# Eight weight buffers as tiles of their own, with 64 bytes between each two

## The chip, the cores and the metric

The kernel runs on one core of a Trainium2 chip, as one launch. The metric is the device time of that launch in microseconds (us), as the median of several runs; smaller is better. A profile is one further execution, taken by the hardware profiler. Engines are named as the profile names them: PE is TensorE's matrix multiply, PEld its weight load, DVE is VectorE, ACT is ScalarE, POOL is GpSimd, SP issues the DMAs.

## The reference

Four layers over 256 tokens of width 1024, batch 1, in float32. Each layer is a half-weighted SwiGLU block, a mixer (three kinds in turn: dilated attention with three groups, differential attention, sliding-window attention with sinks), and a second half-weighted SwiGLU block, each between two RMS norms:

```
def swiglu(x, w_gate, w_up, w_down):
    return (jax.nn.silu(x @ w_gate) * (x @ w_up)) @ w_down

for i in range(DEPTH):                      # DEPTH = 4, D_FF = 2816
    f = swiglu(rms_norm(x, norm_pre[i, 0]), ...)
    x = x + FFN_HALF * rms_norm(f, norm_post[i, 0])
    m = mixer_i(rms_norm(x, norm_pre[i, 1]))
    x = x + rms_norm(m, norm_post[i, 1])
    f = swiglu(rms_norm(x, norm_pre[i, 2]), ...)
    x = x + FFN_HALF * rms_norm(f, norm_post[i, 2])
```

Nearly all arithmetic is in products of the 256 token rows with weights, and every weight is used once per launch.

## The kernel before

**Split products.** Each float32 factor is written as the sum of a high part, rounded to the multiplier's one-pass float32 type, and a low part, the rest. A product then takes three matmuls into the same accumulator: high by high, high by low and low by high (`mm3`, lines 175 to 177). In a matmul one operand is stationary (128 columns, loaded by PEld) and the other streams past it (256, 384 or 512 columns). In the FFN blocks and the output projections the weights stream and the transposed activations are stationary; in the mixers' query and key projections (`qk`) the weights are stationary and the activations stream.

**Weights.** All weights are one list of 377 units of up to 128 x 2048 float32, that is 8 KB per partition each, in the order of use. `load_next` fetches a unit into one of three `raw` buffers by a DMA from SP. `split_next` makes the unit's two parts: ACT copies `raw` into `hi` with rounding (line 142), then DVE subtracts `hi` from `raw` into `lo` (line 143); units in `on_pool` have that subtraction on POOL. A unit is cut into two pieces (four for the first two units and for POOL's). `hi` and `lo` each have four buffers (`AHEAD = 4`). When the last matmul on a unit has been written down, `done` and `pump` split and load the next one, so a unit waits for the buffer of the unit four before it. The framework sets the semaphores, and orders each engine's instructions by the program's order and given priorities.

**Where things lie in SBUF.** Pools follow one another in the order in which they are opened, and in a pool the tags in the order in which they are first asked for. `wp` holds `raw` (3 x 8 KB), `hi` (4 x 8 KB) and `lo` (4 x 8 KB), without gaps. `actp` follows with `x` (8 KB), a gain (4 KB), three work tiles `w` (4 KB each, the transposed probabilities `pw` of the first mixer among them), `xTh` and `xTl` (8 KB each, the transposed input of a block, high and low) and a second gain (4 KB). So all buffers of `raw`, `hi`, `lo`, `xTh` and `xTl` lie whole multiples of 8 KB apart. Behind them the pool `small` has 62 slots of 32 bytes, that is 64 bytes less than a multiple of 512, and then come the block's own tiles: `hTh` and `hTl` (the transposed hidden values, stationary for the down projection `acc`), `oTh` and `oTl`, and the attention's `vh`, `vl`, `q`, `k`. Their distance from `hi`, `lo`, `xTh`, `xTl` and `pw` is therefore 64 bytes off a multiple of 512.

**Names in the profile.** `gu`, `g` and `u` are gate and up projections (weights stream past `xTh`, `xTl`), `acc` the down and output projections (weights stream past `hTh`, `hTl` or `oTh`, `oTl`), `lead` and `v` projections of a mixer with streaming weights, `qk` those with stationary weights. `sc` and `o` are the attention's own products without weights, `tp` a transpose.

Of the kernel before, what the change touches and what calls it, by code (L numbers as in the profile page):

```python
# [8 lines left out]
F32 = mybir.dt.float32  # L9
F32R = mybir.dt.float32r  # L10
# [4 lines left out]
P = 128  # L15
# [9 lines left out]
AHEAD = 4  # L25
# [21 lines left out]
def tile_network(  # L47
# [28 lines left out]
    act, dve, pe, pool = nc.scalar, nc.vector, nc.tensor, nc.gpsimd  # L76

    const = ctx.enter_context(tc.tile_pool(name="const", bufs=1))
    wp = ctx.enter_context(tc.tile_pool(name="wp", bufs=AHEAD))
# [35 lines left out]
    def load_next():  # L115
# [8 lines left out]
            nc.sync.dma_start(out=t[:, c:c + n], in_=units[i][:, c:c + n])  # L124
        raws[i] = t

    def split_next():
        i = state["split"]
        if i >= NU:
            return  # L130
        state["split"] += 1
        w = units[i].shape[-1]
        r = raws.pop(i)
        hi = wp.tile([P, 2048], F32R, tag="hi", name="hi")
        lo = wp.tile([P, 2048], F32R, tag="lo", name="lo")
        eng = pool if i in on_pool else dve
        pieces = 4 if i < 2 or i in on_pool else PIECES
        n = w // pieces
        if True:
            for c in range(pieces):  # L140
                cs = slice(c * n, (c + 1) * n)
                act.copy(out=hi[:, cs], in_=r[:, cs])  # L142
                eng.tensor_tensor(out=lo[:, cs], in0=r[:, cs], in1=hi[:, cs].bitcast(F32), op=ALU.subtract)  # L143
        his[i], los[i] = hi, lo
# [8 lines left out]
    def pump(n=99):  # L153
        while pending and n:
            n -= 1
            i = pending.pop(0)
            split_next()
            load_next()
            for f in hooks.pop(i, []):
                f()  # L160
# [59 lines left out]
    def norm_elem(t, s, parts=1):  # L220

        ss = small.tile([P, 1], F32, tag="ssx", name="ssx")
        hn = actp.tile([P, D], F32, tag="w", name="hn", bufs=3)
        act.activation(out=hn, in_=x[:, t], func=AF.Square, scale=1.0 / 32.0, accum_out=ss)
        r = rstd_of(ss, None)
        for c in range(parts):
            cs = slice(c * D // parts, (c + 1) * D // parts)
            i = dve.scalar_tensor_tensor(out=hn[:, cs], in0=x[:, t, cs], scalar=r, in1=gains["pre", s][:, cs],
                                     op0=ALU.mult, op1=ALU.mult)
        hn_of[t] = hn  # L230
        return i
# [732 lines left out]
    if True:  # L964
# [10 lines left out]
        with tc.high_priority(PRI):  # L975
            i = norm_elem(0, 0, 2)
            j = norm_tr(0)
        with tc.issue_after(i.ins):
            split_next()
# [3 lines left out]
        for _ in range(AHEAD - 1):  # L983
            split_next()
            load_next()
# [158 lines left out]
```

## Time and profile before

| | |
|---|---|
| median of 3 runs | 2353.83 us (2352.81 to 2354.49) |
| the profiled execution | 2352.16 us, of which its span is 2350.3 us |
| granted TensorE clock, mean of the span | 0.991 of full speed |
| PE busy | 2295.6 us (98%), 12922 matmuls |
| weight loads busy | 2016.5 us (86%) |
| DVE, ACT, POOL busy | 1303.9, 1202.3, 619.2 us |
| HBM read | 401.56 MB |

Busy time of PE counts a matmul from its start to its modelled end, and matmuls overlap; the step from one matmul's start to the next one's says more of its pace than its duration does. Idle time of an engine that nobody waits for costs nothing.

### The profile page before, as it was taken

What the parts mean: (1) busy time and instruction counts of PE and PEld (TensorE: products, weight loads), DVE (VectorE), ACT (ScalarE), POOL (GpSimd) and SP (SyncE); (2) the same over time, 40 slices, a digit from 0 to 9 for tenths busy, and PEclk for the clock granted to TensorE, in tenths of its full rate; (3) what the DMA queues carried; (4) which work ended last, traced back from release to release, by engine and by line L of the source; (5) the groups of instructions that cost most, each with busy time, mean ns of one, the idle gap of its engine ahead of it and who ended that gap; (6) DMA issues with size and microseconds to landing.
All of it is one profiled execution on the core that took longest, in us unless ns stands there. A gap on an engine that the chain in (4) does not pass through costs nothing.

```text
span 2350.3 us, 32498 instructions
## 1 busy us (share of the span) xinstructions
PE 2295.6 (98%) x12922; PEld 2016.5 (86%) x12922; DVE 1303.9 (55%) x1914; ACT 1202.3 (51%) x2109; POOL 619.2 (26%) x590
## 2 busy tenths in 40 slices
PE   8999999999999998899999997999999999999998
PEld 6889999988888888788888886788888899998887
DVE  6545444565465558865465459655555544446553
ACT  5435666554444446554454447544444466665442
POOL 0005877620020027520020033100200277774000
PEclk9999999999999999999999998999999999999999
DMA  7544434354554544155555542455455453443542
GB/s 284 194 175 171 168 147 155 140 197 182 187 204 179 182 180 144 73 215 184 192 197 182 189 153 90 161 185 188 168 214 186 173 189 142 146 153 135 215 179 90
DMA packets 60776, 404.71 MB, mean 172 GB/s; under 512 B 7120, under 2 KB 8144, under 8 KB 16592
## 3 DMA queue, kind: packets, MB, share of 16 engines
q1 hardware_dynamic: 60480, 402.57, 46.9%
q8 instruction: 101, 1.65, 0.3%
q14 instruction: 51, 0.42, 0.1%
q10 hardware_dynamic: 144, 0.07, 0.0%
HBM read 401.56 MB, written 1.05 MB: 171 GB/s over the span
## 4 chain that ended last, share of the span: by engine, by line
PE 91%; DVE 6%; ACT 2%; DMA 1%; issue 1%; POOL 0%; SPq 0%; POOLq 0%; DVEq 0%; ACTq 0%
PE gu L177 11%; PE gu L176 11%; PE gu L175 11%; PE acc L175 8%; PE acc L176 8%; PE acc L177 7%; PE qk L175 4%; PE qk L177 4%; PE qk L176 4%; PE v L175 2%; PE v L177 2%; PE v L176 2%; PE tp L367 2%; PE tp L781 1%; PE u L175 1%; PE u L176 1%
## 5 line engine op out<-in xcount | busy, mean ns | idle before, releaser
L142 ACT CAST hi<-raw 128x1024 fp32r<-128x1024 f32 (+2 forms) x970 | 774.5, 843 | 771.7 <-PE gu L177 323.0
L143 DVE TENSOR_TENSOR lo<-raw,hi 128x1024 fp32r<-128x1024 f32 (+1 forms) x546 | 659.5, 1246 | 553.4 <-ACT hi L142 553.2
L143 POOL TENSOR_TENSOR lo<-raw,hi 128x512 fp32r<-128x512 f32 (+1 forms) x424 | 547.0, 1323 | 206.2 <-ACT hi L142 201.6
L175 PE MATMUL gu<-hi,xTh 128*128 128x512 f32 (+1 forms) x1280 | 474.2, 370 | 0.0
L177 PE MATMUL gu<-hi,xTl 128*128 128x512 f32 (+1 forms) x1280 | 471.3, 368 | 0.0
L176 PE MATMUL gu<-lo,xTh 128*128 128x512 f32 (+1 forms) x1280 | 471.0, 368 | 0.0
L213 POOL TENSOR_SCALAR ms<-ssf 128x1 f32<-128x1 f32 x24 | 8.3, 347 | 1413.1 <-ACT junk L242 1410.1
L176 PE MATMUL acc<-lo,hTh 128*128 128x512 f32 x704 | 279.0, 396 | 0.0
L175 PE MATMUL acc<-hi,hTh 128*128 128x512 f32 x704 | 277.1, 394 | 0.0
L177 PEld LDWEIGHTS gu<-hi,xTl 128*128 128x128 f32 x1280 | 241.3, 188 | 40.0
L177 PE MATMUL acc<-hi,hTl 128*128 128x512 f32 x704 | 275.5, 391 | 0.0
L175 PEld LDWEIGHTS gu<-hi,xTh 128*128 128x128 f32 x1280 | 241.4, 189 | 39.3
L176 PEld LDWEIGHTS gu<-lo,xTh 128*128 128x128 f32 x1280 | 241.4, 189 | 39.0
L175 PE MATMUL qk<-xTh,hi 128*128 128x256 f32 x800 | 229.5, 287 | 0.0
L177 PE MATMUL qk<-xTh,lo 128*128 128x256 f32 x800 | 226.6, 283 | 0.0
L176 PE MATMUL qk<-xTl,hi 128*128 128x256 f32 x800 | 226.5, 283 | 0.0
L177 PEld LDWEIGHTS acc<-hi,hTl 128*128 128x128 f32 x704 | 132.2, 188 | 29.9
L175 PEld LDWEIGHTS acc<-hi,hTh 128*128 128x128 f32 x704 | 132.3, 188 | 29.2
L176 PEld LDWEIGHTS acc<-lo,hTh 128*128 128x128 f32 x704 | 132.4, 188 | 26.9
L176 PEld LDWEIGHTS qk<-xTl,hi 128*128 128x128 f32 x800 | 153.4, 192 | 0.0
L177 PEld LDWEIGHTS qk<-xTh,lo 128*128 128x128 f32 x800 | 153.3, 192 | 0.0
L175 PEld LDWEIGHTS qk<-xTh,hi 128*128 128x128 f32 x800 | 153.3, 192 | 0.0
(200 smaller groups left out, 3399.6 us busy)
## 6 DMA issues: line engine op xcount, KB each, us to landing
raw<-in_w_ffn_dram SPq DMA_DIRECT2D x263, 1024.0 KB, 4.8
raw<-in_w_a_qk_dram SPq DMA_DIRECT2D x48, 1024.0 KB, 4.8
raw<-in_w_a_v_dram SPq DMA_DIRECT2D x32, 768.0 KB, 4.3
raw<-in_w_a_out_dram SPq DMA_DIRECT2D x8, 1024.0 KB, 4.8
raw<-in_w_b_qk_dram SPq DMA_DIRECT2D x8, 1024.0 KB, 4.8
gain<-in_g_pre_dram SPq DMA_DIRECT2D x12, 512.0 KB, 6.3
gain<-in_g_post_dram SPq DMA_DIRECT2D x12, 512.0 KB, 8.4
raw<-in_w_b_v_dram SPq DMA_DIRECT2D x4, 1024.0 KB, 4.8
```

The source lines that it names most:

```text
L142: act.copy(out=hi[:, cs], in_=r[:, cs])
L143: eng.tensor_tensor(out=lo[:, cs], in0=r[:, cs], in1=hi[:, cs].bitcast(F32), op=ALU.subtract)
L175: pe.matmul(o, lhsT=a[0], rhs=b[0], start=first, stop=False)
L176: pe.matmul(o, lhsT=a[0], rhs=b[1], start=False, stop=False)
L177: pe.matmul(o, lhsT=a[1], rhs=b[0], start=False, stop=last)
L213: pool.tensor_scalar(out=ms, in0=a, scalar1=b, scalar2=EPS, op0=ALU.add, op1=ALU.add)
L367: pe.transpose(tp[:, i * P:(i + 1) * P], h[:, i * P:(i + 1) * P], ident)
L781: pe.transpose(tp[:, c0:c0 + P], sp[:, i * P:(i + 1) * P], ident)
```

## The change

The four `hi` buffers and the four `lo` buffers stop being slots of two tags and become eight tiles with a tag and a single buffer each, chosen by the unit's number modulo four. When a buffer is first asked for, a 64-byte tile is asked for behind it (16 float32 per partition), and POOL sets it to zero once. Nothing else is edited.

```diff
+    spaces = set()
+
+    def spaced(tag):
+
+        if tag not in spaces:
+            spaces.add(tag)
+            pool.memset(wp.tile([P, 16], F32, tag=tag, name="pad", bufs=1), 0.0)
+
     def split_next():
...
-        hi = wp.tile([P, 2048], F32R, tag="hi", name="hi")
-        lo = wp.tile([P, 2048], F32R, tag="lo", name="lo")
+        b = i % AHEAD
+        hi = wp.tile([P, 2048], F32R, tag=f"hi{b}", name="hi", bufs=1)
+        spaced(f"ph{b}")
+        lo = wp.tile([P, 2048], F32R, tag=f"lo{b}", name="lo", bufs=1)
+        spaced(f"pl{b}")
```

By the order of the tags the eight buffers now lie as hi0, lo0, hi1, lo1 and so on, each 8 KB and 64 bytes behind the one before, and everything behind them moves up by 512 bytes.

## Rows read from the trace of the kernel before

**Rows 1.** The page's head and its first part: busy us, share of the span and instructions of each engine.

```profile
span 2350.3 us, 32498 instructions
...
PE 2295.6 (98%) x12922; PEld 2016.5 (86%) x12922; DVE 1303.9 (55%) x1914; ACT 1202.3 (51%) x2109; POOL 619.2 (26%) x590
```

**Rows 2.** The page's chain of work that ended last, by engine, as shares of the span.

```profile
PE 91%; DVE 6%; ACT 2%; DMA 1%; issue 1%; POOL 0%; SPq 0%; POOLq 0%; DVEq 0%; ACTq 0%
```

**Rows 3.** Who waited for whom: us in total, times, longest us. The first two rows are the longest of all engines that concern the weight buffers; the next two are the first and the last of PE's own 18 rows, none of which names line 142 or 143.

```profile
DVE lo L143 <- ACT hi L142: 553.2, 248, 3.4
ACT hi L142 <- PE gu L177: 323.0, 110, 3.4
```

```profile
PE tp L274 <- DVE hn L228: 11.1, 2, 7.5
...
PE o L175 <- ACT pw L798: 0.3, 1, 0.3
```

**Rows 4.** Groups of PE's instructions by line and shape over the span: count | busy us, mean ns | idle before. One row for each set of three equal ones (lines 175 to 177).

```profile
L175 PE MATMUL gu<-hi,xTh 128*128 128x512 f32 x1024 | 401.1, 392 | 0.0
...
L175 PE MATMUL acc<-hi,hTh 128*128 128x512 f32 x704 | 277.1, 394 | 0.0
...
L177 PE MATMUL qk<-xTh,lo 128*128 128x256 f32 x800 | 226.6, 283 | 0.0
...
L177 PE MATMUL v<-hi,xTl 128*128 128x384 f32 x224 | 75.1, 335 | 0.0
...
L177 PE MATMUL gu<-hi,xTl 128*128 128x256 f32 x256 | 72.4, 283 | 0.0
...
L176 PE MATMUL lead<-lo,xTh 128*128 128x256 f32 x192 | 55.4, 289 | 0.0
...
L177 PE MATMUL acc<-hi,oTl 128*128 128x512 f32 x128 | 50.8, 403 | 0.0
...
L176 PE MATMUL g<-lo,xTh 128*128 128x512 f32 x128 | 50.7, 396 | 0.0
L176 PE MATMUL u<-lo,xTh 128*128 128x512 f32 x128 | 49.9, 390 | 0.0
```

**Rows 5.** Two stretches of 12 steps in the gate and up projections: the engines' busy us and instructions, the granted clock, DMA share and GB/s; then PE's first and last matmul of each stretch, start us and us.

```profile
1533.13:1535.85 2.72, 2.72 (x14) 2.25 (x13) 0.24 (x1) 0.44 (x1) 0.00 (x0) 1.00 0.51 120
709.55:712.27 2.72, 2.72 (x14) 2.25 (x13) 2.12 (x2) 2.01 (x3) 0.00 (x0) 1.00 0.25 105
```

The busy columns are PE, PEld, DVE, ACT, POOL.

```profile
1533.12 0.39 PE L175 MATMUL gu<-hi,xTh 128*128 128x512 f32 x1
...
1535.85 0.39 PE L175 MATMUL gu<-hi,xTh 128*128 128x512 f32 x1
...
709.55 0.39 PE L175 MATMUL gu<-hi,xTh 128*128 128x512 f32 x1
...
712.27 0.39 PE L175 MATMUL gu<-hi,xTh 128*128 128x512 f32 x1
```

**Rows 6.** Two longer unbroken stretches, from the start of the first matmul to the start of the last: `gu` and `acc`, columns as in the group before; then the count of each stretch's matmuls on one of the three lines (32 of 96 in the first, whose last one is counted; 75 of 225 in the second, whose last one begins at its end and is not).

```profile
537.60:559.23 21.63, 21.63 (x98) 17.92 (x97) 11.93 (x12) 9.48 (x12) 0.00 (x0) 1.00 0.48 181
1626.81:1678.40 51.59, 51.59 (x228) 42.35 (x227) 22.61 (x22) 20.42 (x28) 2.61 (x5) 1.00 0.44 159
```

```profile
L175 PE MATMUL gu<-hi,xTh 128*128 128x512 f32 x32 | 12.5, 392 | 0.0
...
L176 PE MATMUL acc<-lo,hTh 128*128 128x512 f32 x75 | 29.5, 394 | 0.0
```

**Rows 7.** PE's instructions in order of time, start us and us: the second and the last of 60 `qk` matmuls in a row, with the count of one of their three lines; then the first and the last of 12 `o` matmuls in a row, in the first and in the seventh of the first mixer's eight groups of heads.

```profile
238.83 0.28 PE L176 MATMUL qk<-xTl,hi 128*128 128x256 f32 x1
...
245.78 0.28 PE L177 MATMUL qk<-xTh,lo 128*128 128x256 f32 x1
...
L176 PE MATMUL qk<-xTl,hi 128*128 128x256 f32 x20 | 5.7, 283 | 0.0
...
261.17 0.28 PE L175 MATMUL o<-pw,vh 128*128 128x256 f32 x1
...
262.42 0.28 PE L177 MATMUL o<-pw,vl 128*128 128x256 f32 x1
...
453.98 0.28 PE L175 MATMUL o<-pw,vh 128*128 128x256 f32 x1
...
455.28 0.28 PE L177 MATMUL o<-pw,vl 128*128 128x256 f32 x1
```

**Rows 8.** POOL's instructions at the start, in order of time: start us, us; then, by groups over the span, one of its clears of a larger tile: count | busy us, mean ns.

```profile
0.33 0.10 POOL L1131 MEMSET const-uint8-127<- 128x1 uint8 x1
0.93 0.20 POOL L969 TENSOR_TENSOR warm<-half 128x1 f32<-128x1 f32 x1 [0.50 <-DVE half L967]
5.74 0.23 POOL L211 TENSOR_SCALAR ms<-ssx 128x1 f32<-128x1 f32 x1 [4.61 <-ACT hn L224]
...
L450 POOL MEMSET dg10h<- 64x256 f32 x2 | 0.6, 310 | 0.1
```

**Rows 9.** Groups by line and shape: the two writers of `lo`.

```profile
L143 DVE TENSOR_TENSOR lo<-raw,hi 128x1024 fp32r<-128x1024 f32 x534 | 648.9, 1254 | 551.5 <-ACT hi L142 551.3
...
L143 POOL TENSOR_TENSOR lo<-raw,hi 128x512 fp32r<-128x512 f32 x304 | 418.1, 1407 | 162.5 <-ACT hi L142 157.8 <-PE tp L781 4.7
```

**Rows 10.** A stretch in the third mixer, columns as in Rows 5.

```profile
1398.00:1500.00 102.00, 84.86 (x460) 71.09 (x461) 85.39 (x210) 71.99 (x186) 36.75 (x32) 0.90 0.29 100
```

## The prediction

> **What bounds the kernel now.** I read the page's head first: PE is busy for 98% of the span and starts 12922 matmuls [rows 1]. Then the chain of waits: PE holds 91% of it, DVE 6%, mostly in the mixers [rows 2]. Then the list of who waited for whom. ACT waits for PE to release a `hi` buffer (323.0 us behind `gu` alone) and DVE waits for ACT, but in PE's own list nothing names line 142 or 143: PE never waited for a split weight [rows 3]. So the weight pipeline is ahead of PE, and the time is PE's own pace plus some waits in the mixers. An edit of the weight buffers can move the time in two ways only: it makes a split weight late, or it changes the step from one matmul to the next.
>
> The steps, then. In `gu` two stretches of 12 steps take 2.73 and 2.72 us, 227 ns a step [rows 5]. At the granted clock of 1.00, the 2.4 GHz level, 512 columns take 213 ns, so 14 ns are spent on something else. Over longer stretches `gu` makes 95 steps in 21.63 us, 227.7 ns, and `acc` 225 in 51.59 us, 229.3 ns, though both stream the same `hi` and `lo` buffers in 512 columns [rows 6]. `qk` makes 58 steps of 256 columns in 6.95 us, 119.8 ns, and `o` 11 steps of 256 columns in 1.25 us, 113.6 ns, or in 1.30 us, 118.2 ns [rows 7]. These differences of a few ns in 120 to 230 are the only place where addresses may hide.
>
> **The change, part by part.** *Four tags instead of four slots.* Units are used, released and split in one order, so a unit's buffer is the one of the unit four before it either way; the waits of ACT on PE stay as they are. I cost this at 0. What covers it is the head start in [rows 3]; were a split late by one piece, it would cost one subtraction, 1.25 us on DVE or 1.41 us on POOL [rows 9], each time PE ran dry, and PE ran dry on a weight not once.
>
> *Eight clears on POOL.* A clear of one element per partition took 0.10 us and one of 64x256 0.31 us, so a 128x16 one lies between: 8 x 0.10 to 8 x 0.31, that is 0.8 to 2.5 us. They read nothing, and POOL idles from 1.13 to 5.74 us [rows 8]. I take 0. If they came behind ACT's first sum and before `ms`, they would push the first norm, and with it all of PE, by up to 2.5 us.
>
> *The moved addresses.* Today `hi`, `lo`, `xTh`, `xTl` lie whole multiples of 8 KB apart. After it, only one of the eight buffers keeps its distance to `xTh` modulo 512 bytes; the others are 64 to 448 bytes off.
>
> Between PE and the engines that write `hi` and `lo`: in one of the two stretches of [rows 5] DVE and ACT are busy for 0.24 and 0.44 of 2.72 us, in the other for 2.12 and 2.01, and the steps agree within the 0.01 us of the listing. With eight buffers on one 8 KB grid a clash would show there. So 0; the bound is 0.01 us in 12 steps, 0.8 ns times 12922, 11 us either way, which nothing in the rows fills.
>
> Inside a writer: DVE reads `raw` and `hi`, which lie on the same grid, and takes 1254 ns for 1024 elements [rows 9]. That may get shorter or longer, but PE does not wait for it [rows 3], so 0.
>
> Inside PE, between the streamed operand and the next weight load: here no row shows the new distances, and I bound from the nearest ones. `acc` is the one place where weights stream beside a stationary operand 64 bytes off the grid, and it is 229.3 - 227.7 = 1.6 ns slower per matmul than `gu`, on the grid. `o` is also 64 bytes off (`pw` streams, `vh` and `vl` are loaded), and is 1.6 to 6.2 ns faster than `qk`, on the grid. So the rows give both signs. Counts, three of each row [rows 4]: on the grid with 512 columns (1024 + 128 + 128) x 3 = 3840, with 256 columns (800 + 256 + 192) x 3 = 3744, with 384 columns 224 x 3 = 672; seven eighths of them change distance: 3360, 3276, 588. Upper end: all 512 and 384 ones go to `acc`'s pace, (3360 + 588) x 1.6 ns = +6.3 us. Lower end: all 256 ones go to `o`'s better pace, 3276 x 6.2 ns = -20.3 us, to its lesser one 3276 x 1.6 = -5.2 us.
>
> I take 0, because of `o`: the first and the seventh group of heads use the very same buffers (24 tiles of `pw` from three slots and six of `v` from two lie between them), and still one steps at 113.6 and the other at 118.2 ns [rows 7]. What precedes a matmul then moves its step by 4.6 ns at equal addresses, more than `acc` and `gu` differ by. `qk` stands ahead of the first, `acc` and `sc` ahead of the other.
>
> The Trainium skill, "TensorE: Matmul & The Clock Gate", section "Back-to-back issue gap", gives 512/2.4 + 2.5 = 216 ns for a lone stream of matmuls at full clock; the trace's 227 is 11 ns longer. In its section on loading the stationary operand it says that TensorE has two independent SBUF read ports and that "Loading the next tile's weights doesn't steal SBUF read bandwidth from the running matmul". By that the 11 ns are not a clash of the two reads, and the change gives 0; by the gap, a clash ended would give 11 ns for each of some 6,300 wide matmuls, an estimate of 70 us.
>
> Sum: 0 on the profiled execution's 2352.16 us (a span of 2350.3 and 1.9 around it). The median of the runs lies 1.7 us above that execution, and I forecast the median: 2353.8 us.
>
> **The rivals.**
> *Slower: weights off the grid stream at `acc`'s pace.* The place is every FFN gate and up projection; the price is 1.6 ns a matmul, from the first matmul whose streamed buffer and next stationary tile no longer agree modulo 512 bytes. For it: `acc` streams the same buffers as `gu`. Against it: `acc` also changes its accumulator every three matmuls, and `o` shows the other sign. Time: 2353.8 + 6.3 = 2360.1, and 2362.6 with the clears at their dearest place on top.
> *Faster: 256-column products at `o`'s pace.* For it: `o` is the fastest 256-column group, 64 bytes off; against it: its two paces at the same addresses. 2353.8 - 5.2 to 2353.8 - 20.3: 2334 to 2349, in the middle 2341. Both rivals at once give 2340 to 2355.
> *Far faster: the 14 ns are a clash of the two reads that the grid forces, and all distances end it.* Then all go to `o`'s excess, 113.6 - 106.7 = 6.9 ns: 512 columns (3840 + (704 + 128) x 3 = 6336) x 7.5 ns = 47.5, 256 columns 3744 x 6.2 = 23.2, together -71 us, 2283. Against it: `acc` is off the grid already and has the larger excess.
> *Waits and clock.* In the mixers the clock falls at times to its lower level of 1.2 GHz: from 1398 to 1500 us 0.90 of it was granted while PE idled in between [rows 10]. Half a microsecond's shift may move such a stretch; I allow 3 us either way, inside the forecast's own band.
> *The change doesn't do what it says*, if the framework lays the small tiles elsewhere: then the distances stay, and the time too. It counts with the forecast.
>
> **How the numbers follow.** Forecast with its band (2349.1 to 2358.5, which is 0.2%, about what a measurement of this kernel can tell from no change): 0.54. Slower by the grid: 0.17; a clear behind the first sum, or a split come late: 0.04. Faster at `o`'s pace: 0.20; far faster: 0.05. That makes faster 0.25, same 0.54, slower 0.21. A range that holds 8 in 10 takes the forecast's band, the slower rival whole and the faster one a little past its middle: 2340 to 2363. Left out are the better half of the faster rival, the far faster one and a wait that nothing shows.
>
> **What would show it.** Right: `gu`, `acc` and `qk` step at 227.7, 229.3 and 119.8 ns over the same counts, PE's list of waits still has no row of line 142 or 143, and the eight clears stand before 5.74 us on POOL. The slower rival: `gu` at 229 ns and `acc` unmoved. The faster one: `qk` at 114 to 118 ns. Wrong altogether: a row in PE's waits that names `hi` or `lo`, or a different order of the splits on ACT.

## The result and the profile after

The changed kernel takes 2387.35 us (median of 4 runs, 2386.89 to 2389.67), the kernel before beside it 2353.48 us: a ratio of 1.0146, 95% interval 1.0128 to 1.0163, so 34 us slower. The forecast was 2353.8, the range ended at 2363. The profiled execution took 2386.89 us, 1.8 of them around its span. Line numbers after the edit are 11 higher: lines 142, 143 and 175 to 177 are now 153, 154 and 186 to 188.

The page's head, its busy times and its chain by engine, of the changed kernel:

```profile
span 2385.1 us, 32506 instructions
...
PE 2319.3 (97%) x12922; PEld 2015.6 (85%) x12922; DVE 1315.0 (55%) x1914; ACT 1201.6 (50%) x2109; POOL 620.0 (26%) x598
...
PE 89%; DVE 7%; ACT 2%; DMA 1%; issue 1%; POOL 0%; SPq 0%; POOLq 0%; DVEq 0%; ACTq 0%
```

Against [rows 1, 2] PE is busy 23.7 us longer with the same 12922 matmuls, DVE 11.1 us longer with the same 1914 instructions, and the chain gives DVE one point more. So there are two places: PE's own pace, and something on DVE.

Who waited for whom in the changed kernel (us in total, times, longest), first the two rows that concern the weight buffers:

```profile
DVE lo L154 <- ACT hi L153: 572.0, 249, 3.4
ACT hi L153 <- PE gu L188: 333.2, 110, 3.6
```

then PE's own list of 19 rows, its first two and its last:

```profile
PE tp L285 <- DVE hn L239: 11.2, 2, 7.6
PE sc L524 <- DVE k L519: 10.0, 2, 6.9
...
PE o L186 <- ACT pw L809: 0.3, 1, 0.3
```

The pipeline of the weights is what it was in [rows 3], with a little more slack, and still no row of PE's list names line 153 or 154. New is the second row: the scores of a mixer waited twice for `k`, 10.0 us in all.

**PE's pace.** The same matmuls as in [rows 6] and the first stretch of [rows 7], found by their place in PE's order (95 steps of `gu`, 225 of `acc`, 58 of `qk`; columns as there):

```profile
541.71:563.79 22.08, 22.08 (x98) 17.93 (x97) 11.92 (x12) 9.46 (x12) 0.00 (x0) 1.00 0.48 174
```

```profile
1649.09:1701.44 52.35, 52.35 (x229) 42.38 (x227) 22.68 (x22) 20.49 (x28) 2.68 (x5) 1.00 0.43 155
242.92:249.73 6.81, 6.81 (x61) 6.81 (x59) 4.70 (x11) 4.37 (x10) 6.64 (x7) 1.00 0.82 267
```

A step of `gu` is 22.08 / 95 = 232.4 ns (227.7 before), of `acc` 52.35 / 225 = 232.7 (229.3), of `qk` 6.81 / 58 = 117.4 (119.8), at the same granted clock of 1.00 and with the other engines as busy as before. Over the whole span, from the starts of all matmuls and leaving out steps over 300 ns, which hold a wait, the means go from 226.9 to 231.6 ns for `gu` with 512 columns, from 229.1 to 232.2 for `acc`, from 227.0 to 231.5 for `u`, and from 121.3 to 120.6 for `qk`. That last mean mixes two levels of the clock: the `qk` steps under 160 ns go from 119.5 to 117.5 ns, but 82 steps of 160 to 300 ns stand in it in place of 50. Matched one to one by name, all steps together (waits included) give `gu` with 512 columns 14.2 us, `acc` 7.1, `u` 1.7 and `g` 1.7: 24.7 of the 34.6 us by which the way from PE's first matmul to its last grew.

**The two holds on DVE.** DVE's and POOL's instructions in order of time (start us, us) at the begin of the second mixer, first in the kernel before, then in the changed one:

```profile
886.99 0.42 DVE L507 TENSOR_TENSOR k<-tp,k 64x256 fp32r<-64x256 f32 x1 [0.82 <-ACT k L506]
887.44 1.27 DVE L508 CAST k<-k 64x512 fp32r<-64x512 f32 x1
```

```profile
879.62 18.33 POOL L143 TENSOR_TENSOR lo<-raw,hi 128x512 fp32r<-128x512 f32 x14 [4.23 <-ACT hi L142]
```

```profile
895.98 0.42 DVE L518 TENSOR_TENSOR k<-tp,k 64x256 fp32r<-64x256 f32 x1 [0.82 <-ACT k L517]
896.43 7.43 DVE L519 CAST k<-k 64x512 fp32r<-64x512 f32 x1
903.78 0.99 DVE L512 SCALAR_TENSOR_TENSOR q<-tp,qsc,q 64x256 fp32r<-64x256 f32 x2
```

```profile
888.62 14.95 POOL L154 TENSOR_TENSOR lo<-raw,hi 128x512 fp32r<-128x512 f32 x12 [4.14 <-ACT hi L153]
```

This copy stacks the key's two parts into the other 64 partitions; undisturbed ones take 0.42 us. Here it ends at 903.86, 0.29 us behind the last of twelve unbroken POOL subtractions (888.62 + 14.95 = 903.57). In the kernel before it asked at the same point of POOL's row (7.82 us behind its begin, here 7.81) and was in after 1.27 us. At the begin of the fourth mixer the same copy takes 7.92 us (0.73 before). In PE's order the steps that wait for these two copies are 6.2 and 5.5 us longer than before (1.6 us of the first came back in a later wait). The granted clock falls behind them, which adds to the price: after PE has stood idle for 6.95 us in the first, `qk` steps take 213 ns in place of 118, and 0.64 is granted in this stretch (columns as in [rows 5]):

```profile
903.50:910.00 6.50, 5.99 (x35) 6.03 (x36) 4.58 (x13) 4.72 (x11) 1.36 (x2) 0.64 0.45 164
```

### The profile page after: what moved, and what is told of

Same layout as the page of the kernel before. It is cut to its first block, busy times and chain, and to the rows that moved or that the text cites. A ratio compares the mean times of both kernels' runs of the same rounds, so it can differ in the third digit from the quotient of the medians.

```text
span 2385.1 us, 32506 instructions
## 1 busy us (share of the span) xinstructions
PE 2319.3 (97%) x12922; PEld 2015.6 (85%) x12922; DVE 1315.0 (55%) x1914; ACT 1201.6 (50%) x2109; POOL 620.0 (26%) x598
## 4 chain that ended last, share of the span: by engine, by line
PE 89%; DVE 7%; ACT 2%; DMA 1%; issue 1%; POOL 0%; SPq 0%; POOLq 0%; DVEq 0%; ACTq 0%
PE gu L188 11%; PE gu L187 11%; PE gu L186 11%; PE acc L186 8%; PE acc L187 8%; PE acc L188 8%; PE qk L187 4%; PE qk L188 4%; PE qk L186 4%; PE v L188 2%; PE v L186 2%; PE v L187 2%; PE tp L378 2%; PE tp L792 1%; DVE lo L154 1%; PE u L186 1%
```

## Experiments: what sets PE's step

Here "distance" is how far the stationary operand begins behind the moving one, counted modulo 256 bytes. In the kernel before it is 0 for `gu` (weights move, `xT` is stationary) and 192 for `acc` (`hT` and `oT` lie 64 bytes short). Behind each time stands its ratio to the kernel before, measured beside it, with the 95% interval in brackets.

**The pads behind the eight buffers.** Tags, clears and the shift of everything behind stay; the buffers lie 8 KB apart again.

```diff
-        spaced(f"ph{b}")
-        spaced(f"pl{b}")
+        if b == AHEAD - 1:
+            for c in range(2 * AHEAD):
+                spaced(f"p{c}")
```

> The changed kernel with its eight pads allocated in one block behind the last low buffer, so that all eight weight buffers lie 8192 bytes apart again (remainder 480 by 512, as the activations), while the eight tags, the eight memsets and the shift of all later tiles by 512 bytes stay. Theory A, the step of TensorE depends on where the two operands lie to each other: gu's 512-column step is back at 226.9 ns, acc's at 229.1, the time at 2353 +- 4 us, with or without a long k<-k copy on VectorE. Theory B, the tags or the memsets cost the time (another release of a buffer, another order): 2380 to 2388 us with gu at 231. Theory C, the shift of the activations by 512 bytes costs it: 2375 to 2388 us with gu at 231.

Measured: 2353.87 us, 1.0001 [0.9992, 1.0011]. The two stretches of `gu` and `acc`:

```profile
538.61:560.24 21.63, 21.63 (x99) 17.92 (x97) 11.93 (x12) 9.48 (x12) 0.00 (x0) 1.00 0.51 178
```

```profile
1629.75:1681.34 51.59, 51.59 (x228) 42.35 (x227) 22.60 (x22) 20.42 (x28) 2.60 (x5) 1.00 0.44 158
```

Both are back to the hundredth (21.63 and 51.59), and no copy is held. The 64 bytes between the buffers make the whole loss; tags, clears and the 512 bytes make none.

**One pad, and everything by 32 bytes.** Two edits of the kernel before: one 64-byte tile behind the weights, and one of 32 bytes ahead of `raw`, which moves all and keeps every distance.

```diff
         lo = wp.tile([P, 2048], F32R, tag="lo", name="lo")
+        if i == 0:
+            pool.memset(wp.tile([P, 16], F32, tag="pad", name="pad", bufs=1), 0.0)
```

```diff
+    pool.memset(wp.tile([P, 8], F32, tag="pad", name="pad", bufs=1), 0.0)
     units = []
```

> The kernel before with one 64-byte tile behind its eight weight buffers: the weights keep 8192 bytes between them, everything behind them moves by 64. Now the transposed activations xT lie 64 bytes off the weights' remainder by 512 (32 against 480), and the hidden activations hT, which lay 64 off it, lie on it (480). Theory A (moving against stationary operand): gu, u and g at 229 to 233 ns (+7 to +20 us), acc at 226.7 (-6 us), the 256-column qk at 117 to 120; time 2352 to 2370 us. Rival, only the distance of the weight buffers to each other (high to low, which follow one another as moving operands) matters: gu stays at 226.9, acc at 229.1, time 2353 +- 3 us.

> The kernel before with one 32-byte tile ahead of the raw buffers: every tile of the weights, the activations and all behind them moves by 32 bytes, all distances stay, and the start of each is a multiple of 64 (remainder 0 by 512 in place of 480). Theory A, only the distances of the operands matter: each step as before, 2353 +- 2 us. Rival, the absolute place matters too (a stream that starts 32 bytes into a 64-byte line): gu off 226.9 by 1 ns or more either way, the time by more than 5 us.

Measured: 2366.59 us, 1.0056 [1.0041, 1.0071], with one pad; 2353.65 us, 1.0002 [0.9993, 1.0011], by 32 bytes. With one pad `gu`, `acc` and `qk`:

```profile
540.29:562.54 22.25, 22.25 (x98) 17.85 (x97) 11.93 (x12) 9.47 (x12) 0.00 (x0) 1.00 0.50 174
```

```profile
1639.38:1690.51 51.13, 51.13 (x228) 42.32 (x227) 22.55 (x22) 20.40 (x28) 2.56 (x5) 1.00 0.45 160
240.41:247.24 6.83, 6.83 (x61) 6.83 (x59) 3.92 (x9) 4.34 (x10) 6.83 (x7) 1.00 0.71 243
```

The weights did not move. `gu`, whose stationary operand moved off, went up to 234.2 ns a step, `acc`, whose stationary operand moved on, down to 227.2, and `qk` down to 117.8. With everything moved by 32 bytes the three means stay within 0.1 ns. So for these steps it is the distance of the two operands, not the place, and not the distance of the buffers to each other alone.

**More distances.** The same tile with 128, 192 or 32 bytes, in the first two with one of 224 bytes in `small` as well, which sets `hT` apart from `xT`; and one with 64 bytes in `small` alone, which puts `hT` to distance 0 too.

```diff
+    pool.memset(small.tile([P, 56], F32, tag="pad", name="pad", bufs=1), 0.0)
     units = []
...
+            pool.memset(wp.tile([P, 32], F32, tag="pad", name="pad", bufs=1), 0.0)
```

> The kernel before with 128 bytes between the weights and the activations and 224 bytes behind the activations: for gu the stationary xT lies 128 bytes from the moving weights (by 256), for acc the stationary hT lies 32 from them. If TensorE's step is a function of that distance alone, repeating by 256 bytes (0: 226.7 ns, 64: 233.4, 192: 229.1 so far), gu has one step of its own for 128 in all its matmuls, between 213 and 237 ns, the same whichever of the eight buffers streams, and acc another for 32. Rival, only a distance of zero is special and all others are alike: gu and acc both at 229 to 234 ns.

> The same with 192 bytes for gu and 96 for acc. If the distance alone decides, gu has here the three steps that acc had at 192 in the kernel before (226, 229 and 232 ns, mean 229.1). Rival, acc's step has another reason (its output in PSUM, its order): gu at 226.7 or at another mean.

> The kernel before with a tile of 32 bytes between the weights and the activations: gu at distance 32, acc at 224. Theory with places of 64 bytes: 32 counts as 0 or as 64, gu at 226.7 or 233.4 ns. Rival, finer places: another step, between 213 and 233 ns.

> The kernel before with one 64-byte tile behind the activations alone, so that hT and oT, 64 bytes off in the kernel before, lie at the weights' remainder, and xT stays on it: gu and acc both at distance 0. Theory: gu stays at 226.9 ns, acc falls from 229.1 to 227.5 or below, as in the run with one pad: 2370 steps x 1.6 to 2.4 ns = -3.9 to -5.7 us, the 256-column o of the weighted sums changes by at most 1.2 us; time 2347 to 2351 us. Rival, the gain of acc is lost in a wait for ScalarE's high parts (PE's steps were hiding it): 2352 to 2355 us with acc's step down all the same.

Measured: 2383.66, 2366.41 and 2376.26 us, one run each; and 2352.91 us, 0.9996 [0.9987, 1.0006], with both at 0. Stretches of `gu` and `acc` at 128 and 32, at 192 and 96, at 32 and 224, in this order:

```profile
543.74:565.89 22.15, 22.15 (x99) 18.00 (x97) 11.93 (x12) 9.46 (x12) 0.00 (x0) 1.00 0.48 175
...
1649.08:1701.66 52.58, 52.58 (x228) 42.39 (x227) 22.72 (x22) 20.50 (x28) 2.69 (x5) 1.00 0.44 155
```

```profile
540.11:561.95 21.84, 21.84 (x98) 17.94 (x97) 11.93 (x12) 9.47 (x12) 0.00 (x0) 1.00 0.52 181
...
1637.10:1689.90 52.80, 52.80 (x228) 42.49 (x227) 22.73 (x22) 20.54 (x28) 2.73 (x5) 1.00 0.43 154
```

```profile
540.99:563.24 22.25, 22.25 (x99) 17.94 (x98) 11.93 (x12) 9.47 (x12) 0.00 (x0) 1.00 0.50 175
...
1644.45:1697.03 52.58, 52.58 (x229) 42.29 (x227) 22.72 (x22) 20.50 (x28) 2.71 (x5) 1.00 0.43 155
```

The means over the span, in ns, with the kernel they come from (steps under 300 ns):

| distance | 512 columns | 256 columns of `gu` |
|---|---|---|
| 0 | 226.9 (`gu`, before); 227.5 (`acc`, one pad) | 120.7 |
| 32 | 233.3 (`gu`); 233.3 (`acc`) | 119.0 |
| 64 | 233.4 (`gu`, one pad) | 114.6 |
| 96 | 234.1 (`acc`) | |
| 128 | 232.6 (`gu`) | 119.6 |
| 192 | 229.0 (`gu`); 229.1 (`acc`, before) | 116.8 |
| 224 | 233.2 (`acc`) | |

Where two kinds of matmul with 512 columns stand at one distance they agree within 0.6 ns, so `acc`'s slower step in the kernel before was its distance, not its accumulators. The kernel before had its widest group, `gu`, at the best of the seven distances tried for 512 columns; 256 columns want another. With `acc` at 0 as well its steps gave 4.0 us, but `o` and `qk` took back 2.0 and 1.9 (`o` went from 115.7 to 120.8 ns: `vh` and `vl` move with `hT`), and the time stayed.

**A mixture, with the measured steps.** In the changed kernel the pads behind the high buffers go; high and low part of a unit then lie alike, the four units at distances 0, 192, 128 and 64 from `xT`.

```diff
-        spaced(f"ph{b}")
```

> The changed kernel with the four pads behind the low buffers alone: high and low part of a unit lie at the same remainder, the units 64 bytes from each other. By 256, xT then lies 0, 192, 128 and 64 from the four, hT 192, 128, 64 and 0. If each step is a function of that distance as the runs have measured it, gu is the mean of 226.8, 229.0, 232.6 and 233.4 = 230.4 ns, buffer by buffer, acc too 230.4 (229.1 before); time 2353.5 + 10.9 (gu) + 3.0 (acc) + 2.6 (u, g) - 2 (256 columns) = 2368 us, 2377 if the two holds come too. Rival, any spacing costs what the change costs: gu at 231.5, acc at 232.2, 2376 to 2388 us.

Measured: 2371.99 us, 1.0074 [1.006, 1.0088]; `gu` 230.8 ns and `acc` 231.1 in the mean, against 230.4 expected for each. By buffer, `gu` takes 227.7 ns in the mean at 0, 229.3 at 192, 232.7 at 128 and 233.4 at 64, the table's values within 1 ns. So the steps add up buffer by buffer where both parts of a unit lie alike. In the changed kernel they do not: the first and the third buffer have `hi` at distance 0 and `lo` at 192, for which the table has 226.9 and 229.0 ns, and the steps of `hi` take 232.2 and those of `lo` 231.3. The two buffers, 256 bytes apart, agree within 0.1 ns on each of the three lines.

So the distance of a matmul's own operands is not all; what runs ahead of it counts too. Two traces show it. In the mixture, units of the first buffer come behind units at distance 64: their fourth to eighth matmul step at 230.8, 228.6, 227.0, 227.8 and 227.1 ns, and only from the eleventh on they stay at 226.5 to 226.8. In the kernel before the fourth to eighth already take 226.5 to 227.0. And `o` (256 columns) behind `qk` has, by the order of the tags, its `pw`, `vh` and `vl` on the very same places in the changed kernel as in the one with the pads behind; only the weights of the `qk` ahead lie elsewhere. Its first and last matmul of 12 in a row, with the pads behind and in the changed kernel:

```profile
262.17 0.28 PE L187 MATMUL o<-pw,vh 128*128 128x256 f32 x1
...
263.41 0.28 PE L189 MATMUL o<-pw,vl 128*128 128x256 f32 x1
```

```profile
265.15 0.28 PE L186 MATMUL o<-pw,vh 128*128 128x256 f32 x1
...
266.45 0.28 PE L188 MATMUL o<-pw,vl 128*128 128x256 f32 x1
```

That is 1.24 against 1.30 us for 11 steps; in the trace's whole ns 113.4 against 117.7 ns a step, in all the 24 rows of `o` behind `qk`.

## Experiments: what holds DVE

**The copy made from PSUM**, first in the changed kernel, then, as a control, in the kernel before:

```diff
-                dve.tensor_copy(out=z[other], in_=z[own])
+                dve.tensor_copy(out=z[other, 0], in_=src[own])
+                dve.tensor_tensor(out=z[other, 1], in0=src[own], in1=z[own, 0].bitcast(F32), op=ALU.subtract)
```

> The changed kernel with the VectorE copy k<-k of 64x512 replaced by a 256-column copy and a 256-column subtraction that read the sum from PSUM and write the other half, so that no two-input-free copy from SBUF to SBUF waits for GpSimd's reads. Theory: the two stalls of 7.4 and 7.9 us are the copy held out by back-to-back GpSimd subtractions; the wait row sc <- DVE k goes, some 9 to 13 us come off: 2374 to 2379 us, gu still at 231.5. Rival, VectorE is held for another reason (its queue, or the tensor_tensor form is held as well): the stall stays on the new instructions and the time within 2384 to 2392 us.

> The kernel before with the k copy alone made from PSUM, as in the changed kernel's run: the control for it. Theory (the edit took 9.4 us off the changed kernel because that kernel has the two long holds, and this one has none): 2351 to 2356 us. Rival (the edit is worth its 9 us anywhere, for the copies of 1.3 to 1.5 us): 2344 to 2349 us.

Measured: 2377.97 us, 1.0102 [1.0085, 1.0118], 9.4 us below the changed kernel; and 2353.99 us, 1.0000 [0.9991, 1.0010], no gain in the kernel before. In the changed kernel with this edit PE's row on `k` is

```profile
PE sc L525 <- DVE k L519: 0.4, 1, 0.4
```

By the medians the two holds cost some 9 of the 34 us and PE's steps some 24. The 9 are a rough figure: the four times of this edit go from 2375.76 to 2383.46 us, and in the slowest of them, the profiled one, four other DVE instructions are held, of which the longest (8.94 us from 1949.37 on) makes `o` wait for 5.8 us. The control shows that a hold needs no spaced buffers: there, on the old places, three other instructions are held for 4.2 to 5.9 us, the one at 1908.10 us among them, and the time is the kernel before's all the same.

```profile
1908.10 5.92 DVE L754 TENSOR_SCALAR sp<-sp,rd 128x512 f32<-128x512 f32 x1
```

**POOL's row moved away**: in the changed kernel POOL begins three units later, so DVE makes those low parts itself.

```diff
-            on_pool.update(range(ids[5 if kind == 0 else 4], ids[-1] + 5))
+            on_pool.update(range(ids[{0: 8, 1: 7, 2: 4}[kind]], ids[-1] + 5))
```

> The changed kernel with GpSimd's first units in the mixers three units later (in the first two kinds), so that VectorE makes those low parts itself and no row of twelve GpSimd subtractions runs where the two copies are held; places unchanged. Theory, GpSimd's unbroken row is the holder: no k<-k copy over 3 us, the wait row of sc on DVE k under 2 us; time 2374 to 2382 us (24.5 us of the steps stay; VectorE's three more units per mixer may cost some). Rival, VectorE is held by something else: a copy of 7 us stays, 2385 to 2390 us.

Measured: 2374.15 us, 1.0087 [1.0072, 1.0103], with `gu` still at 231.6 ns. In place of twelve subtractions from 888.62 on POOL makes three, and the copies beside them take 1.1 to 1.3 us:

```profile
896.54 3.96 POOL L154 TENSOR_TENSOR lo<-raw,hi 128x512 fp32r<-128x512 f32 x3 [13.51 <-ACT hi L153]
```

```profile
896.97 1.13 DVE L519 CAST k<-k 64x512 fp32r<-64x512 f32 x1
899.46 1.32 DVE L519 CAST k<-k 64x512 fp32r<-64x512 f32 x1
```

No copy of the kernel takes longer than 1.5 us, and the time is 13.2 us below the changed kernel's; the two edits together put the holds at 9 to 13 us. POOL's unbroken row is the holder: all 16 DVE instructions over 3 us in the traces of these kernels end within 0.3 us of the end of such a row.

**When the copy asks.** A VectorE memset ahead of each copy, in both kernels (shown for the changed one; the kernel before sets a scratch tile of its own), and then the subtraction ahead of the copy made twice, in the changed kernel.

```diff
+                dve.memset(spaces["ph0"], 0.0)
                 dve.tensor_copy(out=z[other], in_=z[own])
```

```diff
                 dve.tensor_tensor(out=z[own, 1], in0=src[own], in1=z[own, 0].bitcast(F32), op=ALU.subtract)
+                dve.tensor_tensor(out=z[own, 1], in0=src[own], in1=z[own, 0].bitcast(F32), op=ALU.subtract)
```

> The changed kernel, all places as they are, with one VectorE memset of 128x16 ahead of each k<-k copy, so that the copy asks some 60 to 100 ns later. Theory, whether the copy gets in between two back-to-back GpSimd subtractions is a matter of the instant at which it asks: the holds of 7.4 and 7.9 us at 896 and 1922 us go or change (one or both copies under 2 us), others may come; time 2374 to 2384 us if they go. Rival, the places of the tiles make the hold: both holds stay within 0.5 us, time 2386 to 2390.

> The kernel before with the same memset ahead of each k<-k copy (its scratch tile of 256 bytes moves hT and all behind it by 256). Theory, the instant decides: a hold of several us may now come here too, with the weights on their old places; if one comes 2356 to 2362 us, if none 2353 +- 2. By the theory that the distance counts by 256 bytes acc stays at 229.1 ns with hT at a remainder of 160 by 512 in place of 416; if it counted by 512 it would change by over 1 ns (3 to 12 us). Rival for the holds, the places make them: none here, and no copy over 1.6 us.

> The changed kernel with the subtraction ahead of each k<-k copy made twice, so that the copy asks 0.45 us later (the memset of the run before had run ahead of the subtraction and had not moved the copy). Theory, the instant decides whether the copy gets in: at least one of the two holds goes (under 2 us), 2374 to 2384 us; others may come. Rival, the place decides: both stay, each some 0.45 us shorter since they end when GpSimd's row ends, 2385 to 2391 us.

Measured: 2386.74 us, 1.0151 [1.0131, 1.0171], and 2354.20 us, 1.0002 [0.9992, 1.0011], with the memset; 2402.14 us, 1.0204 [1.0190, 1.0218], with the second subtraction. The memset told nothing about the instant: it depends on nothing, the framework put all 50 into the first 27 us of the launch, and the copy asked as before, 0.46 us behind the subtraction's start. What the pair is good for: the holds come back in another execution at the same two copies (7.42 and 7.97 us), and `acc` stays at 229.2 ns with `hT` 256 bytes further on, so the distance counts by 256. With the second subtraction both holds stay, 7.82 and 7.80 us, and a third of 7.81 us comes at 229.5 us, in the first mixer, and another instruction is held for 8.23 us. Neither theory has it right: the tiles did not move and a hold came, so places alone do not decide; the copies asked later and two holds stayed, so it is no near miss at those two. In the mixture above one of the two came (7.44 us) and the other not (1.58 us). The spacing seems to have a part in it: in the 11 traces with the weight buffers 8 KB apart and this copy in place none takes over 1.6 us, and all four with spaced buffers, the copy and POOL's row have one, two or three held. What lets the copy in between two subtractions stays open.

## Places chosen by the measured steps

The kernel before, with `xT`'s tiles 256 bytes longer so that the view begins 192 bytes in for the mixers, and the feed-forward's `hT` 64 bytes later. In the first of two runs `hTl` lay 64 bytes too far, in the second it lies right; the edit shown is the second's. In `qk` the weights are the stationary operand, so its distance is then 64, at which the 256 columns of `gu` had their best step.

```diff
+        off = 48 if xT.get("n", 0) % 3 == 1 else 0
+        xT["n"] = xT.get("n", 0) + 1
+        for c in "hl":
+            z = actp.tile([P, KD * SEQ + 64], F32R, tag="xT" + c, name="xT" + c)
+            xT[c] = z[:, off:off + KD * SEQ].rearrange("p (k n) -> p k n", k=KD)
...
+            hTh = fp.tile([P, KF * SEQ + 16], F32R, name="hTh", bufs=1)[:, 16:].rearrange("p (k n) -> p k n", k=KF)
```

> The kernel before with the operands placed stage by stage: xT's two tiles have 256 bytes to spare, in the mixers its view begins 192 bytes in (distance 192, where the 256-column qk ran at 118.5 in place of 121.3 ns), in the feed-forward stages at 0 (gu at 226.8); the feed-forward stages' hT begins 64 bytes later (acc there at 0), the mixers' oT and all else stay as in the kernel before. Theory, the gains add: qk -5 to -6.6 us, acc -3 to -4 us, lead and v within 1 us: 2342 to 2347 us. Rival, part of it goes into waits: 2347 to 2352; no gain: 2353 and above.

> The run by stages with hT's low half on the weights' remainder as well (there it lay 64 bytes further by mistake, and acc rose to 231.0 ns): acc of the feed-forward stages at distance 0 in both halves, xT at 192 in the mixers. Theory: acc at 227.5, that is 3.5 ns x 2368 = 8.3 us below the run by stages: 2339 to 2343 us. Rival, waits eat part: 2343 to 2349.

Measured: 2348.96 us, 0.9979 [0.9970, 0.9989], with `acc` at 231.0 ns from `hTl`'s 64 bytes; then 2342.78 us, 0.9952 [0.9940, 0.9965], faster than both kernels. `qk` went from 121.3 to 117.1 ns in the mean (-9.7 us) and `acc` from 229.1 to 227.6 (-3.7 us), while `gu` stayed:

```profile
533.88:555.51 21.63, 21.63 (x98) 17.93 (x97) 11.93 (x12) 9.48 (x12) 0.00 (x0) 1.00 0.50 180
```

```profile
1620.55:1671.68 51.13, 51.13 (x229) 42.32 (x227) 22.57 (x22) 20.40 (x28) 2.56 (x5) 1.00 0.43 158
```

## Why the prediction was wrong

*Inside PE, between the streamed operand and the next weight load: "I take 0, because of `o`".* This step failed, by 24.7 us. Its premise is right: what runs ahead moves a step at equal addresses, as the two paces of `o`, 113.6 and 118.2 ns, say [rows 7], and the same `o` shows it again, 113.4 with the pads behind and 117.7 in the changed kernel. What failed is the conclusion, that an effect of this size leaves none to the places. In `gu`, where nothing but `gu` runs ahead, the two stretches [rows 5] agreed to 0.01 us, and there one pad of 64 bytes moves the mean step by 6.5 ns. The paces of `o` hang on its distance too: with `vh` at distance 0 both groups take 119.5 to 120.0 ns.

*The bound "all 512 and 384 ones go to `acc`'s pace", +6.3 us.* The slower rival had place and sign right and the size wrong: 1.6 ns were taken for any distance, measured were 4.7 for `gu` (231.6 - 226.9). `acc`'s distance, the only other one in the trace, is the mildest of the six tried besides 0; the rest cost 5.7 to 7.2 ns. And "`acc` unmoved" was wrong: its own distances changed, and it lost 3.1 ns a step. A single row off the grid bounds nothing from above. The count was off too: modulo 256 bytes two of the eight buffers keep their distance to `xT`, not one, and they got slower all the same (232.2 ns for the steps of `hi`), since their `lo` had moved.

The Trainium skill, "TensorE: Matmul & The Clock Gate", section "Step-by-step: what each phase is for", was the other support: two independent read ports, so that loading the next stationary operand takes nothing from the running matmul, hence no cost. The measurement decides: whatever the mechanism, which no run here names, the step depends on where the two operands lie to each other.

*"That may get shorter or longer, but PE does not wait for it".* This looked at DVE and POOL only as writers of `lo`. There the step was right (1253 ns and 1410 ns for the pieces of [rows 9]). The mixers' own DVE instructions share time with POOL's row, and no part of the sum had them: 9 to 13 us, outside the 3 us allowed for waits and clock. [rows 2] gave the hint, 6% of the chain on DVE.

The Trainium skill, "SBUF — State Buffer", section "Who interferes with whom", says that a VectorE copy in its two-port mode and GpSimd exclude each other, the later one waiting for the whole of the other's instruction. The copy of 1.27 us in the kernel before, in behind the subtraction that was running, agrees. The one of 7.43 us agrees in that it waits entirely, but not that it waits for one instruction: it sits out the rest of one subtraction and five more. Which mode the copy runs in no run shows.

*Four tags, 0*: right, as the run with the pads behind shows. *Eight clears, 0*: right; they stand ahead of `ms` as supposed, and take 0.40 us together:

```profile
0.72 0.40 POOL L133 MEMSET pad<- 128x16 f32 x8 [0.29 <-POOLq L1142]
1.16 0.19 POOL L980 TENSOR_TENSOR warm<-half 128x1 f32<-128x1 f32 x1
5.73 0.23 POOL L222 TENSOR_SCALAR ms<-ssx 128x1 f32<-128x1 f32 x1 [4.38 <-ACT hn L235]
```

*Faster at `o`'s pace*: this rival was right for `qk`, whose stretch went to 117.4 ns and whose steps under 160 ns went from 119.5 to 117.5, some 4.7 us over 2347 steps. The mean over all falls by 0.7 ns only, for more `qk` steps stand at the lower clock behind the holds. The 256 columns of `gu` did not move (120.7 and 120.6 ns), and `o` itself went from 115.7 to 118.6.

## What to carry to other kernels

When PE runs back to back with a new stationary operand for each matmul, as it does here, the addresses of the two operands are a parameter like a tile size: look at the step from start to start in a steady row, vary one operand's place by 32 to 192 bytes, keep parts that stream in turn at one remainder, and choose per stage, since 512 and 256 columns wanted different distances here. Change such places on purpose only; a small tile put in anywhere moves everything behind it. And where POOL works off a long row of tensor instructions, look which DVE copies fall into it and who waits for them.

## What was not expected of the hardware

- The step of the same 512-column matmul at the granted clock of 1.00 ran from 226.9 to 234.1 ns by distance, that of 256 columns from 114.6 to 120.7, in the opposite order at 64 bytes; 32 bytes of shift of everything changed nothing.
- The distance counts modulo 256 bytes (`acc` at 229.1 and 229.2 ns with `hT` 256 bytes apart), and with high and low part 64 bytes apart a matmul at distance 0 loses its good step (232.2 in place of 226.9 ns).
- The step keeps a memory of what ran ahead: a whole row of 12 matmuls on unmoved operands took 113.4 or 117.7 ns a step.
- A DVE copy of 0.42 us was held for 7.4 to 8.0 us until POOL's row of 12 or 13 subtractions had ended, in some runs and places, and in others got in after one.
